# A decoder trunk's second mixer: GLA's core in batches of two token tiles and ahead of its gate, the output projection in three parts, fewer weight chunks completed by transfer

## The chip, the core and the metric

The kernel runs on one core of a Trainium2 chip. The metric is the device time of one execution in microseconds (us). TensorE (PE) multiplies, VectorE (DVE), ScalarE (ACT) and GpSimd (POOL) compute, SyncE (SP) issues most DMAs. Each engine takes its instructions strictly in the order in which the program lists them, and waits at the first one that isn't ready.

## What is computed

512 tokens of width 1024 go through two layers. Each layer is half a feed-forward block, a mixer, and another half of a feed-forward block, each added to the scaled input and layer-normed:

```python
for l in range(DEPTH):                      # DEPTH = 2, D_MODEL = 1024, D_FF = 2816
    x = layer_norm(alpha * x + 0.5 * swiglu_ffn(x, ffn1_wi[l], ffn1_wo[l]), ...)
    mix = even_mixer(x, ...) if l % 2 == 0 else odd_mixer(x, ...)
    x = layer_norm(alpha * x + mix, ...)
    x = layer_norm(alpha * x + 0.5 * swiglu_ffn(x, ffn2_wi[l], ffn2_wo[l]), ...)
```

The change is in the second layer's mixer. Its input projection feeds two groups of heads of 512 features each, RWKV-7 and GLA; their results are put side by side and multiplied by one 1024 x 1024 output matrix:

```python
def odd_mixer(x, w_in, w_out, ...):
    p = (x @ w_in).astype(jnp.float32)
    p_rk, p_gla = p[..., :RK_IN], p[..., RK_IN:]
    y_rk = rwkv7_mixer(p_rk, ...)           # per token: state <- state*w + ..., y = state @ r
    gq, gk, gv, ggd, gog = split_cols(p_gla, GLA_SIZES)
    y_gla = gla_mixer(gq, gk, gv, ggd, gog, ...)
    return jnp.concatenate([y_rk, y_gla], axis=-1).astype(x.dtype) @ w_out

def gla_mixer(q, k, v, gd, og, gB, gb, norm_g):
    log_alpha = jax.nn.log_sigmoid(gd @ gB + gb) / GLA_TAU
    ...                                     # chunks of 64 tokens, 4 heads
    attn = jnp.where(causal, einsum(q_dec, k_inv), 0.0)
    o = einsum(attn, v)
    ...
    def step(state, inp):                   # 8 chunks, one after the other
        dec, kv_c = inp
        return dec[..., None] * state + kv_c, state
    o = o + einsum(q_dec, s_prev)
    return head_norm(o, norm_g, None, GLA_NORM_EPS) * jax.nn.silu(og)
```

## The kernel before

**Products.** All large products keep float32 accuracy with three matmuls in fp32r: an operand is split into a high part and the remainder, and `hi*hi`, `lo*hi` and `hi*lo` are summed in PSUM. x is kept transposed and split as `xh` and `xl` (`hi_lo()`: ACT L166 copies the high part, DVE L167 subtracts).

**Weights.** They are streamed in chunks of 512 KB. `load()` has SP bring a chunk into `raw` (two buffers, L87). `split()` turns it into `whi` and `wlo` (five buffers): ACT L99 copies the high part, and the remainder is made in one of two ways. Normally DVE L103 subtracts. While the flag `adds` is set, which is the whole of the second mixer, ACT L101 instead writes minus the high part's source into `wlo` and POOL issues a second, accumulating transfer of the same chunk on top of it (L106), so DVE has nothing to do for it. `weights()` splits two chunks ahead of the one in use. The second mixer's chunks come in this order: `lora` (0), `gd` (1), the RWKV-7 keys, receptances and values by feature tile (2 to 13, `od_krv`), GLA's keys and queries (14 to 17), its values (18 to 21), its gate (22 to 25), and the output matrix (26 to 33, `od_w_out`).

**The second mixer, `odd(l)`.** First the projections `pj` for chunks 0 to 4 run over the tokens of the first half, then, after the last token tile is normed and transposed (`to_xT(3)`), over the second half. RWKV-7's 512 features are four tiles of 128 in two groups of two. A group goes through `keys` (gates `pw`, `pa`, norms `pn`, the bonus `pi`), `scores` (`psc`), `inverse` (a triangular inverse that DVE works out in 15 x 2 steps, L789 and L790, between block transposes L785 and L796), `natural` (transposes `ptk`, `ptb` and products `pz` on PE), `merge` (`pq`, `px`, `pwt`, `pu`: the inverse is applied; it needs the finished inverse) and `chain` (eight chunks of 64 tokens one after the other: PE `psa` L847, DVE L848, PE `pst` L854, DVE L856 and L859). `finish` norms the results and multiplies by the gate (`pyt`).

**What fills the waits.** Around these, `filler` holds a queue of generators, and `fill()` advances it by counts from the table FILL; `drain()` empties it. The first group's steps are filled with the other projections, `gla_gates`, `gla_kq` and `gla_v` (PE tile `pv`). For the second group the queue before is `gla_o` (GLA's output gate: 96 matmuls of 512 columns into `po`, then ACT L964 and DVE L965, L966 make `og`), then `gla_core` (for each of the four token tiles in turn: transposes `ptk` L992, scores `psc` L1000, a masked copy L1002 on DVE, chunk states `pkv` L1013 with DVE L1016 and L1017, outputs `po` L1023 and L1026, and their `head_norm`), then `values` (L1037 multiplies by `og`; L1040 transposes into `xh`, `xl`). A scheduler then sets the final order on each engine.

**Output projection.** `MixOut` takes the features by tiles of 128: 0 to 3 RWKV-7, 4 to 7 GLA. In each part it multiplies the tiles of that part for every token tile (PE `pout`, L161 to L163, 512 columns each) and adds the result to x on DVE (L1134 in part 0, which also scales x; L1136 in later parts). Part 0 runs as filler of the second chain; the last part, `mix.last`, also does the layer norm (L192, L194, L200, L202) and transposes x for the next block (`pst` L174, L166, L167), whose first matmul is `pgu` L128.

```python
mix = MixOut(self, (0, 1, 4), (5, 6, 7, 2, 3))
```

PSUM has eight banks: four of tag A, two of B, two of C.

Of the kernel before, what the change touches and what calls it, by code (L numbers as in the profile page):

```python
# [23 lines left out]

FILL = (
# [3 lines left out]
)  # L29


class Net:
    def __init__(self, ctx, tc, a):
# [57 lines left out]
    def split(self):  # L91
# [5 lines left out]
        for z in range(0, n, 512):  # L97
            sl = slice(z, min(n, z + 512))
            self.nc.scalar.activation(hi[:, sl], t[:, sl], AF.Copy)  # L99
            if self.adds and not fold:  # L100
                self.nc.scalar.activation(lo[:, sl], t[:, sl], AF.Copy, scale=-1.0)  # L101
            elif not fold:
                self.nc.vector.tensor_tensor(out=lo[:, sl], in0=t[:, sl], in1=hi[:, sl].bitcast(F32), op=ALU.subtract)  # L103
        if self.adds and not fold:
# [446 lines left out]

    def odd_srcs(self):
        a = self.a
        self.srcs.append((a["od_lora"][0], (8, P), 0))
        self.srcs.append((a["od_gd"], (8, 48), 32))
        for nm in ("od_krv", "od_gkq", "od_gv", "od_go"):
            for q in range(a[nm].shape[0]):
                self.srcs.append((a[nm][q], tuple(a[nm].shape[2:]), 0))
        self.out_srcs(a["od_w_out"][0], (0, 1, 4, 5, 6, 7, 2, 3))

    def odd(self, l):
        nc, a, tc = self.nc, self.a, self.tc
        V, A, T, G = nc.vector, nc.scalar, nc.tensor, nc.gpsimd
        self.adds = True
# [5 lines left out]
        with tc.tile_pool(name="od", bufs=1) as ep:  # L570
# [400 lines left out]
            def gla_start():  # L971
                nc.sync.dma_start(ng, a["gla_norm_g"].broadcast_to([P, S]))
                V.tensor_scalar(out=ng, in0=ng, scalar1=0.5, scalar2=None, op0=ALU.mult)
                at = [gp.tile([P, 2, P], F32, name=f"at{z}") for z in range(4)]
                for z in range(4):
                    G.memset(at[z], 0.0)
                return at

            qd, ki = Es, gbs

            def gla_core():
                St = gp.tile([P, 2, P], F32, name="Sg", bufs=3)
                V.memset(St, 0.0)
                for t in range(4):
                    St = yield from gla(t, St)

            def gla(t, St):
                ts = slice(t * P, (t + 1) * P)
                heads = [(f, par, slice(par * 64, par * 64 + 64), f * 256 + par * P) for f in range(2) for par in range(2)]
                p = self.psum("ptk", "A")  # L990
                for f in range(2):
                    T.transpose(p[:, f * P:(f + 1) * P], ki[f][:, ts], self.ident)  # L992
                kn = gp.tile([P, 2, P], F32, name="kn")
                A.activation(kn, p[:, :256].rearrange("p (f i) -> p f i", f=2), AF.Copy)
                yield
                pp = [self.psum("psc", "A") for _ in range(2)]
                for f in range(2):
                    for par, p in enumerate(pp):
                        rows = slice(par * 64, par * 64 + 64)
                        T.matmul(p[:, f * P:(f + 1) * P], ki[f][rows, ts], qd[f][rows, ts], start=True, stop=True)  # L1000
                for par, p in enumerate(pp):
                    V.copy_predicated(out=at[t % 2 * 2 + par], mask=m_gla.bitcast(mybir.dt.uint32).unsqueeze(1).broadcast_to([P, 2, P]), data=p[:, :256].rearrange("p (f i) -> p f i", f=2))  # L1002
                yield
                po = [self.psum("po", "A") for _ in range(2)]
                ss = []
                for z in range(2):
                    c = 2 * t + z
                    rows = slice(z * 64, z * 64 + 64)
                    ss.append(St)
                    if c < 7:  # L1010
                        p = self.psum("pkv", "A")
                        for f, par, q, i in heads:
                            T.matmul(p[q, f * P:(f + 1) * P], kn[rows, f, q], vt[t][rows, i:i + P], start=True, stop=True)  # L1013
                        pv = p[:, :256].rearrange("p (f i) -> p f i", f=2)
                        Sn = gp.tile([P, 2, P], F32, name="Sg", bufs=3)
                        V.tensor_tensor(out=Sn, in0=pv, in1=St, op=ALU.add)  # L1016
# [3 lines left out]
                for f in range(2):  # L1020
                    two = [(po[par][:, f * P:(f + 1) * P], par, q, i) for g, par, q, i in heads if g == f]
                    for o, par, q, i in two:
                        T.matmul(o, at[t % 2 * 2 + par][:, f, :], vt[t][:, i:i + P], start=True, stop=False)  # L1023
                    for z in range(2):
                        for o, par, q, i in two:
                            T.matmul(o[z * 64:z * 64 + 64], qd[f][q, t * P + z * 64:t * P + z * 64 + 64], ss[z][q, f, :], start=False, stop=True)  # L1026
                sm = ep.tile([P, 48], F32, name="sm", bufs=2)
                y = slot("kr")
                head_norm(sm, [(po[h % 2][:, h // 2 * P:(h // 2 + 1) * P], y[:, h * P:(h + 1) * P]) for h in range(4)], 1e-5)
                yg.append(y)  # L1030
                yield
                return St


# [65 lines left out]

            filler.append(mix_first())
            for t, y in enumerate(chain(grp)):
# [4 lines left out]
            for q in later:  # L1107
                rk_values(*q)
            gp.release()
            self.adds = False  # L1110
            mix.last(l, lambda nm: slot("y" if nm != "lnt" else "kr"))


# [159 lines left out]
```

## Time and profile before

| | |
|---|---|
| median of 3 runs | 2036.09 us (2035.59 to 2046.99) |
| the profiled execution | 2039.38 us, of which the span is 2037.6 us |
| PE busy in the span | 2003.2 us (98%) |
| DVE, ACT, POOL busy | 966.1 us (47%), 716.7 us (35%), 95.1 us (5%) |
| mean granted PE clock | 0.991 |
| second mixer | from about 1320 us to 1667 us of the span |

The page has one row of busy time for each engine, the span in 40 slices (the second mixer is in slices 26 to 33, counted from 1), and the chain that ended last, with the share of each engine and line. Views for a stretch of time give each engine's busy time there, the granted PE clock, which falls from 1.00 to 0.50 in places, and the DMA engines' share. A row of waits names the PE line that waited, the engine and line it waited for, the total in us, how often, and the longest.

### The profile page before, as it was taken

The numbers are of one execution on the slowest core, as the hardware profiler recorded it, in microseconds if no ns is written. First come the engines' busy times: TensorE is split into PE (matmuls) and PEld (weight loads), VectorE is DVE, ScalarE is ACT, GpSimd is POOL, SyncE is SP. The second block draws the span as 40 slices with busy tenths as digits, with TensorE's granted clock in tenths as the row PEclk, the third lists the DMA queues.
The fourth block names the chain that finished last, engine by engine and source line by source line (L and its number), as shares of the span: only waits on it lengthen the run. The fifth ranks groups of instructions, "written<-read, shape, count | busy, mean of one in ns | idle before, by whom it ended". The sixth has DMA issues, their size and how long they took to land.

```text
span 2037.6 us, 26047 instructions
## 1 busy us (share of the span) xinstructions
PE 2003.2 (98%) x10485; PEld 1661.1 (82%) x10485; DVE 966.1 (47%) x1800; ACT 716.7 (35%) x1264; POOL 95.1 (5%) x157
## 2 busy tenths in 40 slices
PE   9999999999999999999999999998999999999998
PEld 8888888876888888888988888886777788888886
DVE  4332333766784323336433333436857784323335
ACT  4332331456433322332332233166535333322330
POOL 0000000100010000000000000012111200000001
PEclk9999999999999999999999999998998999999999
DMA  5233332322223233232333332285536023333331
GB/s 177 93 101 117 95 102 83 98 93 63 72 93 115 93 97 121 93 97 65 118 99 97 114 103 94 77 213 114 132 81 157 20 84 114 96 101 114 99 98 63
DMA packets 60635, 206.64 MB, mean 101 GB/s; under 512 B 7953, under 2 KB 8417, under 8 KB 60513
## 3 DMA queue, kind: packets, MB, share of 16 engines
q1 hardware_dynamic: 56336, 189.77, 29.8%
q0 software_dynamic: 4176, 15.21, 4.0%
q8 instruction: 82, 1.34, 0.3%
q14 instruction: 41, 0.33, 0.1%
HBM read 200.75 MB, written 4.19 MB: 101 GB/s over the span
## 4 chain that ended last, share of the span: by engine, by line
PE 90%; DVE 4%; ACT 3%; DMA 2%; issue 1%; POOL 0%; POOLq 0%; SPq 0%; DVEq 0%; ACTq 0%
PE pgu L128 16%; PE pgu L129 16%; PE pgu L132 16%; PE acc L163 8%; PE acc L162 8%; PE acc L161 8%; PE pout L161 1%; PE pout L162 1%; PE pout L163 1%; DMA raw<-od_krv 1%; PE pv L152 1%; PE pst L174 1%; PE pj L128 1%; ACT whi L99 1%; PE pv L154 1%
## 5 line engine op out<-in xcount | busy, mean ns | idle before, releaser
L99 ACT ACTIVATE whi<-raw 128x512 fp32r<-128x512 f32 x661 | 380.3, 623 | 839.6 <-PE pgu L129 403.4
L103 DVE TENSOR_TENSOR wlo<-raw,whi 128x512 fp32r<-128x512 f32 x600 | 388.4, 687 | 533.4 <-ACT whi L99 507.8
L128 PE MATMUL pgu<-xh,whi 128*128 128x512 f32 (+1 forms) x1568 | 563.1, 368 | 1.5 <-ACT whi L99 1.3
L129 PE MATMUL pgu<-xl,whi 128*128 128x512 f32 (+1 forms) x1568 | 564.0, 368 | 0.0
L132 PE MATMUL pgu<-xh,wlo 128*128 128x512 f32 (+1 forms) x1568 | 353.6, 367 | 0.0
L128 PEld LDWEIGHTS pgu<-xh,whi 128*128 128x128 f32 x1568 | 294.2, 188 | 50.5 <-ACT whi L99 1.5
L129 PEld LDWEIGHTS pgu<-xl,whi 128*128 128x128 f32 x1568 | 295.2, 188 | 48.6
L132 PEld LDWEIGHTS pgu<-xh,wlo 128*128 128x128 f32 x1568 | 275.7, 189 | 48.6
L161 PE MATMUL acc<-whi,hh 128*128 128x512 f32 x704 | 274.4, 390 | 0.0
L162 PE MATMUL acc<-whi,hl 128*128 128x512 f32 x704 | 274.2, 389 | 0.0
L163 PE MATMUL acc<-wlo,hh 128*128 128x512 f32 x704 | 272.3, 390 | 0.0
L239 DVE TENSOR_TENSOR sg<-sg,pgu 128x512 f32<-128x512 f32 (+1 forms) x96 | 61.7, 643 | 335.6 <-PE pgu L132 331.4
L162 PEld LDWEIGHTS acc<-whi,hl 128*128 128x128 f32 x704 | 132.2, 188 | 27.3
L161 PEld LDWEIGHTS acc<-whi,hh 128*128 128x128 f32 x704 | 132.2, 188 | 27.2
L163 PEld LDWEIGHTS acc<-wlo,hh 128*128 128x128 f32 x704 | 132.1, 188 | 27.2
L166 ACT ACTIVATE hh<-sg 128x512 fp32r<-128x512 f32 (+1 forms) x96 | 57.3, 596 | 121.5 <-DVE sg L239 121.5
L196 POOL TENSOR_SCALAR rs<-mv 128x1 f32<-128x1 f32 x24 | 13.7, 571 | 1507.5 <-DVE mv L194 1507.5
L238 ACT ACTIVATE sg<-pgu 128x512 f32<-128x512 f32 (+1 forms) x96 | 53.7, 560 | 56.0 <-PE pgu L132 55.4
L128 PE MATMUL pj<-xh,whi 128*128 128x512 f32 (+2 forms) x184 | 65.4, 372 | 0.0
L166 ACT ACTIVATE xh<-pst 128x512 fp32r<-128x512 f32 x48 | 27.5, 596 | 106.6 <-PE pst L174 106.5
L129 PE MATMUL pj<-xl,whi 128*128 128x512 f32 (+2 forms) x184 | 62.7, 357 | 0.0
L167 DVE TENSOR_TENSOR hl<-sg,hh 128x512 fp32r<-128x512 f32 (+1 forms) x96 | 61.6, 641 | 0.6 <-ACT hh L166 0.5
(342 smaller groups left out, 2006.5 us busy)
## 6 DMA issues: line engine op xcount, KB each, us to landing
raw<-ffn_wi SPq DMA_DIRECT2D x176, 512.0 KB, 3.5
raw<-ffn_wo SPq DMA_DIRECT2D x88, 512.0 KB, 3.5
raw<-od_krv SPq DMA_DIRECT2D x12, 512.0 KB, 4.6
wlo<-od_krv POOLq DMA_DIRECT2D x12, 512.0 KB, 7.6
raw<-ev_qk SPq DMA_DIRECT2D x8, 512.0 KB, 3.5
raw<-ev_rg SPq DMA_DIRECT2D x8, 512.0 KB, 3.4
raw<-ev_w_out SPq DMA_DIRECT2D x8, 512.0 KB, 3.5
raw<-od_w_out SPq DMA_DIRECT2D x8, 512.0 KB, 4.2
```

The costliest lines, as they stand in the source:

```text
L99: self.nc.scalar.activation(hi[:, sl], t[:, sl], AF.Copy)
L103: self.nc.vector.tensor_tensor(out=lo[:, sl], in0=t[:, sl], in1=hi[:, sl].bitcast(F32), op=ALU.subtract)
L128: mm(o, hi[:, kt, :n], self.xh[:, kt, t0:t1], start=kt == 0, stop=False)
L129: mm(o, hi[:, kt, :n], self.xl[:, kt, t0:t1], start=False, stop=lo is None and kt == 7)
L132: mm(o, lo[:, kt, :n], self.xh[:, kt, t0:t1], start=False, stop=kt == 7)
L161: mm(o, ah, hi[:, cs], start=first and i == 0, stop=False)
L162: mm(o, al, hi[:, cs], start=False, stop=False)
L163: mm(o, ah, lo[:, cs], start=False, stop=last and i == len(lhs) - 1)
L166: self.nc.scalar.activation(hi, src, AF.Copy)
L167: self.nc.vector.tensor_tensor(out=lo, in0=src, in1=hi.bitcast(F32), op=ALU.subtract)
L238: nc.scalar.activation(sg, pp[f, 0][:, t0:t1], AF.Silu)
L239: nc.vector.tensor_tensor(out=sg, in0=sg, in1=pp[u][:, t0:t1], op=ALU.mult)
```

## The change

It has three parts, all in the second mixer.

- `gla_core` works on two token tiles at a time: one `ptk` bank for four transposes, two `psc` banks for sixteen scores, masked copies of 512 columns in place of 256, two `pkv` banks that hold all four chunk states of the batch, then the two tiles' outputs. `filler` takes `gla_core`, then `gla_o`, then `values`, all queued behind the second group's `inverse`; the count at that place of FILL is 22 in place of 19, and later counts change too.
- The output projection has three parts: tiles (0, 1, 4), then (5, 6, 7), then (2, 3). The first two are filler of the second chain.
- `adds` is a range of chunk numbers in place of a flag: chunks 8 to 31 of the second mixer are completed by transfer. Chunks 2 to 7 (`od_krv` for the first two feature tiles) and the last two of the output matrix are subtracted on DVE. Before, the flag was set when `odd` began and cleared before `mix.last`: 2 to 7 were completed by transfer, and of the output matrix chunks 26 to 30. As built, the adding transfers of `od_krv` go from 12 to 6 and L101 on `od_w_out` covers one chunk more.

```diff
-    3, 1, 2, 2, 3, 2, 1, 3, 2, 1, 0, 1, 1, 3, 0, 0, 6, 3, 3, 5, 6, 4, 2, 9, 0, 1, 19, 8, 0, 1, 4, 2,
-    1, 3, 1, 0, 1, 2, 2, 3, 1, 4, 0, 1, 1, 1, 2, 0, 1,
+    3, 1, 2, 2, 3, 2, 1, 3, 2, 1, 0, 1, 1, 3, 0, 0, 6, 3, 3, 5, 6, 4, 2, 9, 0, 1, 22, 6, 6, 2, 2, 2,
+    2, 1, 1, 1, 1, 1, 1, 1, 1, 1, 1, 1, 1, 1, 1, 1, 1,
...
-            if self.adds and not fold:
+            if self.nsp in self.adds and not fold:
                 self.nc.scalar.activation(lo[:, sl], t[:, sl], AF.Copy, scale=-1.0)
...
     def odd_srcs(self):
+        n = len(self.srcs)
+        self.adds = range(n + 8, n + 32)
...
-                for t in range(4):
-                    St = yield from gla(t, St)
+                for t0 in (0, 2):
+                    St = yield from gla(t0, St)
+            def gla(t0, St):
+                ts = [slice((t0 + i) * P, (t0 + i + 1) * P) for i in range(2)]
                 p = self.psum("ptk", "A")
+                for i in range(2):
+                    for f in range(2):
+                        T.transpose(p[:, (2 * i + f) * P:(2 * i + f + 1) * P], ki[f][:, ts[i]], self.ident)
...
                 for par, p in enumerate(pp):
+                    V.copy_predicated(out=at[par], mask=m_gla..., data=p.rearrange("p (t f i) -> p t f i", t=2, f=2))
                 yield
+                pp = [self.psum("pkv", "A") for _ in range(2)]
...
+                for c in range(2 * t0, 2 * t0 + 4):
                     ss.append(St)
                     if c < 7:
+                        V.tensor_tensor(out=Sn, in0=pp[z][:, i * 256:i * 256 + 256]..., in1=St, op=ALU.add)
                         V.tensor_tensor(out=Sn, in0=Sn, in1=Dg[...], op=ALU.mult)
                         St = Sn
...
-            mix = MixOut(self, (0, 1, 4), (5, 6, 7, 2, 3))
+            mix = MixOut(self, (0, 1, 4), (5, 6, 7), (2, 3))
...
-            filler += [gla_o()]
+            filler += [gla_core(), gla_o(), values()]
             fill()
-            filler += [gla_core(), values()]
             merge(grp)
...
-                yield from mix.part(0, "A")
+                for i in range(2):
+                    yield from mix.part(i, "A")
...
-            self.adds = False
```

**PE beside the second inverse.** Before, PE has the gate's matmuls (`po<-whi,xh` and its two companions) between the transposes and `pz` products of `natural`. These rows are from the middle of that stretch:

```order
L154 MATMUL po<-wlo,xh 128x512
L773 MATMUL pz<-KV,SC 64x64 x16
L759 MATMUL ptk<-ident,KRV 128x128 x4
L152 MATMUL po<-whi,xh 128x512
L153 MATMUL po<-whi,xl 128x512
```

In the changed kernel the core's batches stand there (L994, L1003, L1015, L1032, L1036). This is the beginning of the second batch:

```order
L994 MATMUL ptk<-ident,ga 128x128 x4
L1003 MATMUL psc<-E_10211,ga 128x128
L1003 MATMUL psc<-E_10212,ga 128x128
L1003 MATMUL psc<-E_10211,ga 128x128
L1003 MATMUL psc<-E_10212,ga 128x128
L1003 MATMUL psc<-E_10211,ga 128x128
L1003 MATMUL psc<-E_10212,ga 128x128
L1003 MATMUL psc<-E_10211,ga 128x128
L1003 MATMUL psc<-E_10212,ga 128x128
L1015 MATMUL pkv<-kr,kn 64x128 x16
L1032 MATMUL po<-kr,at_11717 128x128
L1036 MATMUL po<-Sg,E_10211 64x128
```

Behind those twelve rows stand ten `pq`, then the rest of that batch's outputs, twenty-one `pq`, and only then the gate's matmuls; `gla_o`'s 96 matmuls have moved from beside the inverse to behind it.

**DVE at the second inverse.** Before, its 30 steps (L789, L790) stand nearly one behind the other (between them are two L167 and two memsets). In the changed kernel L790 and L791 are the same steps, and the core's instructions stand between them, here from the middle:

```order
L790 TENSOR_TENSOR ZU<-ZU 64x210
L1022 TENSOR_TENSOR Sg<-pkv,Sg 128x256
L791 TENSOR_TENSOR ZU<-ZU 64x10x21
L1023 TENSOR_TENSOR Sg<-Sg,Dg 128x256
L790 TENSOR_TENSOR ZU<-ZU 64x198
L1022 TENSOR_TENSOR Sg<-pkv,Sg 128x256
L883 BN_STATS sm<-po 128x6 x3
```

The second batch's masked copies are the two L1005 at the end of the inverse, one ahead of its last step and one behind its three closing transposes (L794 and L797):

```order
L1005 COPY_PREDICATED at_11717<-cst,psc 128x512
L791 TENSOR_TENSOR ZU<-ZU 64x30
L794 STREAM_TRANSPOSE WT<-ZU 32x32x32
L797 STREAM_TRANSPOSE SC<-ZU 32x32x32 x2
L1005 COPY_PREDICATED at_11718<-cst,psc 128x512
L1022 TENSOR_TENSOR Sg<-pkv,Sg 128x256
L1023 TENSOR_TENSOR Sg<-Sg,Dg 128x256
```

So the whole first batch's DVE work, and one of the second's copies, have moved into the inverse.

**PE in the second chain.** Before, a step of the chain from `psa` to the next `psa` is filled with GLA's core and transposes of its results:

```order
L847 MATMUL psa<-St,WT 64x128
L1040 MATMUL pyt<-ident,kr 128x128 x4
L854 MATMUL pst<-KV,BK 128x128 x2
L870 MATMUL py<-KV,SC 64x64 x3
L866 MATMUL py<-St,R 64x128 x2
L870 MATMUL py<-KV,SC 64x64 x4
L1040 MATMUL pyt<-ident,kr 128x128 x4
```

In the changed kernel nine `pout` stand between `psa` (L848 there) and `pst` (L855), and eight or nine behind the `py` of each token tile:

```order
L848 MATMUL psa<-St,WT 64x128
L161 MATMUL pout<-whi,xh 128x512
L162 MATMUL pout<-whi,xl 128x512
L163 MATMUL pout<-wlo,xh 128x512
L161 MATMUL pout<-whi,xh 128x512
L162 MATMUL pout<-whi,xl 128x512
L163 MATMUL pout<-wlo,xh 128x512
L161 MATMUL pout<-whi,xh 128x512
L162 MATMUL pout<-whi,xl 128x512
L163 MATMUL pout<-wlo,xh 128x512
L855 MATMUL pst<-KV,BK 128x128 x2
```

Between the last product of the last chunk (`py`, L870 before, L871 after) and the first `pgu` of the next block, 161 `pout` remain before and 74 after.

More of the change, by code (lines that the diff above doesn't have):

```diff
@@ L54, in __init__ @@
         self.raw = {}
-        self.adds = False
+        self.adds = range(0)
         self.spl = {}
@@ L103, in split @@
                 self.nc.vector.tensor_tensor(out=lo[:, sl], in0=t[:, sl], in1=hi[:, sl].bitcast(F32), op=ALU.subtract)
-        if self.adds and not fold:
+        if self.nsp in self.adds and not fold:
             self.nc.gpsimd.dma_start(lo[:, :n].rearrange("p (a b) -> p a b", a=shape[0]), ap, accum_op=ALU.add)
@@ L973, in gla_start @@
                 V.tensor_scalar(out=ng, in0=ng, scalar1=0.5, scalar2=None, op0=ALU.mult)
-                at = [gp.tile([P, 2, P], F32, name=f"at{z}") for z in range(4)]
-                for z in range(4):
-                    G.memset(at[z], 0.0)
+                at = [gp.tile([P, 2, 2, P], F32, name=f"at{par}") for par in range(2)]
+                for par in range(2):
+                    G.memset(at[par], 0.0)
                 return at
@@ L996, in gla @@
                 pp = [self.psum("psc", "A") for _ in range(2)]
[L997 to L1000, printed above, removed]
+                for i in range(2):
+                    for f in range(2):
+                        for par, p in enumerate(pp):
+                            rows = slice(par * 64, par * 64 + 64)
+                            T.matmul(p[:, (2 * i + f) * P:(2 * i + f + 1) * P], ki[f][rows, ts[i]], qd[f][rows, ts[i]], start=True, stop=True)
@@ L1001, in gla @@
                 for par, p in enumerate(pp):
[L1002 removed]
+                    V.copy_predicated(out=at[par], mask=m_gla.bitcast(mybir.dt.uint32).unsqueeze(1).unsqueeze(1).broadcast_to([P, 2, 2, P]), data=p.rearrange("p (t f i) -> p t f i", t=2, f=2))
                 yield
[L1004 removed]
+                pp = [self.psum("pkv", "A") for _ in range(2)]
@@ L1005, in gla @@
+                for i in range(2):
+                    for f in range(2):
+                        for par in range(2):
+                            for z, p in enumerate(pp):
+                                rows, q = slice(z * 64, z * 64 + 64), slice(par * 64, par * 64 + 64)
+                                j = f * 256 + par * P
+                                T.matmul(p[q, (2 * i + f) * P:(2 * i + f + 1) * P], kn[rows, i, f, q], vt[t0 + i][rows, j:j + P], start=True, stop=True)
                 ss = []
-                for z in range(2):
-                    c = 2 * t + z
-                    rows = slice(z * 64, z * 64 + 64)
+                for c in range(2 * t0, 2 * t0 + 4):
@@ L1009, in gla @@
                     ss.append(St)
                     if c < 7:
[L1011 to L1016, printed above, removed]
+                        i, z = (c - 2 * t0) // 2, c % 2
@@ L1017, in gla @@
+                        Sn = gp.tile([P, 2, P], F32, name="Sg", bufs=5)
+                        V.tensor_tensor(out=Sn, in0=pp[z][:, i * 256:i * 256 + 256].rearrange("p (f i) -> p f i", f=2), in1=St, op=ALU.add)
                         V.tensor_tensor(out=Sn, in0=Sn, in1=Dg[:, :, c:c + 1].broadcast_to([P, 2, P]), op=ALU.mult)
                         St = Sn
-                    yield
[L1020 to L1031, printed above, removed]
+                yield
+                for i in range(2):
+                    po = [self.psum("po", "A") for _ in range(2)]
+                    for f in range(2):
+                        two = [(po[par][:, f * P:(f + 1) * P], par, slice(par * 64, par * 64 + 64)) for par in range(2)]
+                        for o, par, q in two:
+                            j = f * 256 + par * P
+                            T.matmul(o, at[par][:, i, f, :], vt[t0 + i][:, j:j + P], start=True, stop=False)
+                        for z in range(2):
+                            for o, par, q in two:
+                                u = (t0 + i) * P + z * 64
+                                T.matmul(o[z * 64:z * 64 + 64], qd[f][q, u:u + 64], ss[2 * i + z][q, f, :], start=False, stop=True)
+                    sm = ep.tile([P, 48], F32, name="sm", bufs=2)
+                    y = slot("kr")
+                    head_norm(sm, [(po[h % 2][:, h // 2 * P:(h // 2 + 1) * P], y[:, h * P:(h + 1) * P]) for h in range(4)], 1e-5)
+                    yg.append(y)
+                    yield
@@ L1098, in mix_first @@
                     rk_values(i, slice(0, S))
-                yield from mix.part(0, "A")
+                for i in range(2):
+                    yield from mix.part(i, "A")
             filler.append(mix_first())
@@ L1109, in odd @@
             gp.release()
-            self.adds = False
             mix.last(l, lambda nm: slot("y" if nm != "lnt" else "kr"))
```

12 lines of the change are left out of this document (3 added, 9 removed).

## The prediction

> **What bounds the kernel now.** I start with the page's busy times and chain.
>
> ```profile
> PE 2003.2 (98%) x10485; PEld 1661.1 (82%) x10485; DVE 966.1 (47%) x1800; ACT 716.7 (35%) x1264; POOL 95.1 (5%) x157
> PE 90%; DVE 4%; ACT 3%; DMA 2%; issue 1%; POOL 0%; POOLq 0%; SPq 0%; DVEq 0%; ACTq 0%
> ```
>
> TensorE is the bound nearly everywhere. The change neither adds nor removes PE work: the same matmuls come in another order. So it can only move time in which PE idles or runs slowly. I therefore look for these in the second mixer, first from the last key score of the second group (1526.85, called T0) to the next block's first `pgu` (1667.10): beside the inverse, behind it, in the chain, and in the tail. Columns: length, then busy us of PE, PEld, DVE, ACT and POOL with their instructions, granted clock, DMA share, GB/s.
>
> ```profile
> 1526.85:1537.91 11.06, 11.06 (x55) 9.16 (x55) 10.36 (x23) 5.47 (x11) 0.86 (x1) 1.00 0.32 71
> 1537.91:1562.20 24.29, 24.29 (x229) 20.00 (x228) 22.05 (x49) 15.90 (x29) 4.27 (x8) 1.00 0.84 198
> 1562.20:1580.60 18.40, 16.13 (x247) 12.61 (x240) 9.12 (x15) 7.16 (x14) 1.08 (x2) 0.72 0.50 154
> 1580.60:1624.30 43.70, 40.54 (x376) 30.33 (x374) 32.23 (x121) 15.68 (x41) 11.95 (x28) 1.00 0.07 15
> 1624.30:1667.10 42.80, 42.25 (x199) 34.12 (x199) 34.05 (x73) 11.52 (x25) 5.87 (x10) 1.00 0.15 50
> ```
>
> PE is busy throughout the inverse's 35.35 us. In all 140.25 us it idles 2.27 + 3.16 + 0.55 = 6.0 us. Second, the granted clock, in windows of the same kind:
>
> ```profile
> 1339.50:1342.90 3.40, 1.31 (x11) 1.10 (x10) 1.55 (x6) 1.57 (x4) 1.39 (x2) 1.00 1.04 277
> 1342.90:1346.30 3.40, 3.40 (x18) 3.38 (x18) 0.13 (x2) 0.00 (x0) 0.00 (x0) 0.50 1.06 251
> 1383.90:1387.30 3.40, 1.12 (x2) 0.29 (x2) 3.30 (x6) 3.40 (x8) 0.93 (x1) 1.00 0.41 119
> 1387.30:1394.10 6.80, 6.16 (x12) 3.79 (x13) 5.85 (x10) 4.13 (x8) 1.16 (x2) 0.50 1.03 243
> 1418.00:1424.80 6.80, 6.58 (x26) 5.99 (x27) 5.98 (x8) 5.04 (x11) 2.01 (x3) 0.50 0.53 119
> 1561.40:1564.80 3.40, 1.64 (x90) 1.42 (x84) 2.84 (x4) 1.07 (x2) 0.86 (x1) 0.99 1.02 358
> 1564.80:1575.00 10.20, 10.20 (x98) 7.65 (x93) 3.44 (x5) 2.79 (x5) 0.00 (x0) 0.50 0.47 132
> 1611.00:1614.40 3.40, 2.15 (x16) 1.58 (x15) 2.11 (x7) 3.20 (x10) 1.80 (x5) 1.00 0.02 5
> 1614.40:1617.80 3.40, 3.40 (x23) 2.65 (x21) 3.34 (x19) 1.19 (x4) 2.20 (x6) 1.00 0.00 0
> ```
>
> Where PE is busy 1.1 to 1.6 us of a window of 3.4, the clock is 0.50 for the next 3.4 to 10.2 us; after 2.15 us it stays. Half of such a stretch is lost: 1.7, 3.4, 3.4 and 5.1 us at the four places. With the second half's idle time that makes 6.0 + 5.1 = 11.1 us lost there. Third, PE's waits from 1330 to 1425:
>
> ```profile
> PE pn L701 <- ACT wk L697: 3.4, 2, 2.5
> PE pw L688 <- DVE wk L728: 2.2, 1, 2.2
> PE pj L132 <- DMA wlo<-od_krv: 2.1, 1, 2.1
> PE pa L692 <- ACT wk L690: 1.6, 1, 1.6
> PE pi L726 <- ACT wk L724: 0.8, 1, 0.8
> ```
>
> **The change part by part: chunks 2 to 7.** Twelve L101 on ACT and six accumulating transfers go; twelve L103 on DVE come.
>
> ```profile
> wlo<-od_krv POOLq DMA_DIRECT2D x12, 512.0 KB, 7.6
> raw<-od_krv SPq DMA_DIRECT2D x12, 512.0 KB, 4.6
> L101 ACT ACTIVATE wlo<-raw 128x512 fp32r<-128x512 f32 x26 | 15.5, 618 | 0.0
> L103 DVE TENSOR_TENSOR wlo<-raw,whi 128x512 fp32r<-128x512 f32 x600 | 388.4, 687 | 533.4 <-ACT whi L99 507.8
> ```
>
> The DMA engines are full in the first window (share 1.04), and each remainder lands 7.6 us after its issue. Without six of them the `pj` wait of 2.1 us ends, and with it the half clock behind it (1.7). ACT gets 12 x 0.618 = 7.4 us back, and its chain of gates feeds `pa`, `pi` and `pn`: 1.6 + 0.8 + 0.9 (of the two `pn` waits the shorter). If these go, the window at 1383.90 no longer idles and 3.4 us of half clock go too. The wait of `pw` is on DVE, which gets 12 x 0.687 = 8.2 us more; its 2.2 us may go, because the weights come earlier, or stay. In sum 2.1 + 1.7 + 1.6 + 0.8 + 0.9 + 3.4 = 10.5 without `pw`, 12.7 with it. The longer `pn` wait (2.5) and the half clock at 1418 lie behind the third feature tile's gates, whose chunks are still completed by transfer; they stay. I take **-10.5**. The ends: -16 if that stall halves too (2.5 + 3.4, by half: 3.0), and -3 if only the `pj` wait goes because DVE's 8.2 us come late for the gates.
>
> **GLA's core under the inverse.** The inverse is DVE's:
>
> ```profile
> L790 DVE TENSOR_TENSOR ZU<-ZU 64x30 f32<-64x30 f32 (+14 forms) x30 | 9.9, 330 | 1.0
> L789 DVE TENSOR_TENSOR ZU<-ZU 64x30 f32<-64x30 f32 (+14 forms) x30 | 9.9, 329 | 1.0
> L1002 DVE COPY_PREDICATED at<-cst,psc 128x256 f32<-128x256 uint32 x8 | 3.2, 439 | 1.6 <-PE psc L1000 1.5
> L1016 DVE TENSOR_TENSOR Sg<-pkv,Sg 128x256 f32<-128x256 f32 x7 | 2.9, 420 | 1.1 <-PE pkv L1013 1.0
> L882 DVE BATCH_NORM_STATS2 sm<-po 128x6 f32<-128x128 f32 x16 | 3.7, 286 | 2.6 <-PE po L1026 2.4
> L884 DVE BATCH_NORM_AGGREGATE sm<-sm 128x2 f32<-128x6 f32 x28 | 3.0, 154 | 0.0
> ```
>
> Inserted ahead of its end are three masked copies of twice 256 columns (3 x 0.75, an estimate between 0.44 and 0.88), four pairs of L1022 and L1023 (8 x 0.42, starts some 0.36 apart), eight norm statistics (8 x 0.286, starts 0.22 apart) and eight aggregates (8 x 0.154): 2.2 + 2.9 + 1.8 + 0.9, about 7.6 us with their rounding. DVE stood idle 35.35 - 10.36 - 22.05 = 2.9 us there, of which I let 2.4 take some up. The inverse ends 7.6 - 2.4 = 5.2 us later, at T0 + 40.5.
>
> PE meanwhile loses its cover:
>
> ```profile
> L152 PE MATMUL po<-whi,xh 128*128 128x512 f32 x27 | 10.8, 401 | 0.0
> L1023 PE MATMUL po<-kr,at 128*128 128x128 f32 x32 | 6.4, 307 | 0.0
> L1026 PE MATMUL po<-Sg,E 64*64 64x128 f32 x64 | 5.3, 294 | 0.0
> ```
>
> 81 of `gla_o`'s 96 matmuls ran there, at 0.2275 us from start to start (an estimate: 10.8 us of L152 alone counts overlap): 18.4 us. In their place come batch one and batch two as far as the first ten `pq`, which wait for the inverse: by the rows above half of 6.4 + 5.3 and the scores, states and transposes, 13.2 us with the waits inside a batch. So PE has 35.35 - 18.4 + 13.2 = 30.2 us of work, 28.2 when I walk the starts one by one, against 40.5. It idles **12.3** (10.3 by the first count). Then batch two's outputs must be normed before the gate's PSUM banks come free: another **3.4** (one aggregate, POOL's four small steps and ACT's scaling take about 2 us). After such idling the clock halves for at least the 3.4 us of the shortest row, up to 10.2: 1.7 to 5.1 lost, I take **2.6**. `og` and `values` come in one burst on DVE ahead of the chain's first operand: four L965, L966 and L1037 of 0.69 us each, 8.3 us of DVE, against PE with only `pyt` left to do: **3.2** idle.
>
> **The chain and the tail.** With nine `pout` (nine times 0.2275, 2.0 us) between `psa` and `pst`, the chain's waits on DVE and ACT vanish and PE is busy there. But 87 `pout` (161 less 74), 19.8 us, have gone from the tail:
>
> ```profile
> L162 PE MATMUL pout<-whi,xl 128*128 128x512 f32 x54 | 21.4, 396 | 0.0
> L1136 DVE TENSOR_TENSOR x<-x,pout 128x512 f32<-128x512 f32 x7 | 4.7, 682 | 1.4 <-PE pout L163 1.4
> L192 DVE BATCH_NORM_STATS2 st<-x 128x6 f32<-128x512 f32 x7 | 4.7, 688 | 0.1
> L200 DVE SCALAR_TENSOR_TENSOR kr<-x,mv,y 128x512 f32<-128x512 f32 x6 | 4.2, 748 | 0.1
> L202 DVE SCALAR_TENSOR_TENSOR x<-kr,rs,y 128x512 f32<-128x512 f32 x6 | 4.5, 747 | 0.9 <-POOL rs L197 0.9
> ```
>
> DVE was busy 34.05 of that stretch's 42.80 us, and the third part adds eight more additions of 0.68 to it or to the chain. Per token tile the tail has two each of L1136, L192, L200, L202 and L167, about 7.3 us; four tiles make 29, with `finish` of the last tile and the next block's L103 35 us. PE has 42.25 - 19.8 - 1.5 (what moved over the border) = 20.9 us to do. The tail takes 35 us and PE idles **14**.
>
> **Sum.** Second half: lost after 12.3 + 3.4 + 2.6 + 3.2 + 14 = 35.5, before 11.1: **+24** (from +14, where the inverse is lengthened by only 2 and the tail takes 29, to +34, with 10.2 us windows of half clock twice and a tail of 40). With the first half 24 - 10.5 = +13.5, so 2039.38 + 13.5 = 2052.9 for the profiled execution (its span of 2037.6 and 1.8 around it). That one lies 3.3 above the median of the runs; against the median I say **2050**.
>
> A rule of the Trainium skill bears on this. "TensorE: Matmul & The Clock Gate", section "What's actually happening", has the clock fall to half after an idle window of about 3.4 us and come back after a busy one. The windows above agree on the length and on 0.50, but here 1.1 to 1.6 us of work did not prevent it. Read strictly, the page's rule would spare the tail, where no idle piece is that long (14 us in four tiles, about 3.5 each and in pieces): by it the time stays at 2050, by the falling rows it is the first rival's.
>
> **Rivals.** *The tail runs at half clock* (slower). PE would be busy 20.9 of 35 us, 2.03 us in a window of 3.4: between the rows that fall (1.64) and the row that stays (2.15). If it falls, the 20.9 us become up to 41.8, more than DVE's 35: the tail is 6.8 longer, and the next `pgu` begin with 3.4 us at 0.50 (1.7), and the longer half clock behind the inverse adds 2.5. Price 11, **2061**. It decides from 2.03 being above or below the gate's point, which lies between 1.64 and 2.15. *The first half gains nothing*: the waits of `pa`, `pi`, `pn` hang on chains through DVE, which has 8.2 us more to do; only the `pj` wait goes: 2050 + 7.5 = **2057.5**. *DVE is less in the way* (no slower): GLA's operations fit between the inverse's dependent steps, and the tail keeps up with its additions at 29 us. The second half is then +14 or less, the first -10.5 to -16: 2036 + 14 - 10.5 = 2039.6 down to **2034**. *PE never waits for DVE* (faster): nothing is idle in the second half (-11.1), the first gives -12.7: **2012**. The inverse with DVE busy 32.4 of 35.35 us speaks against it. *The change does not do what it says*: the rows of the order do show it.
>
> **How the numbers follow.** Forecast 2050 (2043 to 2056): 0.46. Tail at half clock 0.20, first half without gain 0.10, DVE less in the way 0.17, PE never waiting 0.07. One per cent is 20.4 us, about what a measurement of this kernel can tell from no change: 2015.7 and 2056.5. Faster by more: 0.07. Slower by more: the tail's 0.20, half of the 0.10 and 0.04 of the forecast's upper edge: 0.29. Between: 0.64. The range leaves out PE never waiting and the far ends of both sides: 2030 to 2066.
>
> **What would show it.** Right: PE idle for some 10 to 12 us near T0 + 28 waiting for the inverse's transposes, the first `gla_o` matmul near T0 + 48, no wait of `pj` on `od_krv`, no half clock at 1387, chain waits near nothing, a tail of 35 us with DVE over 90% busy, and T0 to `pgu` about 164. Wrong: PE busy beside the inverse, a tail under 25 us, or first-half waits that merely change names.

## The result and the profile after

The changed kernel takes 2064.01 us (median; 2059.75 to 2066.45) against 2040.62 us (2035.59 to 2046.99) in the runs beside it. The ratio is 1.0105, 95% interval 1.0075 to 1.0135: about 1% slower. The profiled execution took 2066.45 us with a span of 2064.7; before, 2039.38 and 2037.6. Two executions of the later runs, 7135 us of the kernel before and 2222 us of adds_dense, were slow at mean granted clocks of 0.267 and 0.845 and are in none of the ratios.

The page of the changed kernel, busy times and chain:

```profile
PE 2024.0 (98%) x10493; PEld 1676.9 (81%) x10493; DVE 978.0 (47%) x1814; ACT 711.6 (34%) x1252; POOL 89.5 (4%) x150
PE 88%; DVE 6%; ACT 2%; DMA 2%; issue 1%; POOL 0%; POOLq 0%; DVEq 0%; SPq 0%; ACTq 0%
```

PE is busy 20.8 us longer with the same work, which is the sign of a slower clock rather than of waiting (the mean granted clock is 0.982, 0.991 before); DVE's share of the chain has gone from 4% to 6%. The changed kernel's second half, in windows as before: `pv` to T0 + 10.8, the inverse, batch two's outputs, the gate and merge, the chain, the tail, and the first 22.9 us of the next block:

```profile
1523.90:1534.70 10.80, 10.80 (x55) 8.94 (x55) 10.10 (x23) 5.45 (x10) 0.86 (x1) 1.00 0.35 73
1534.70:1566.70 32.00, 26.14 (x262) 19.49 (x260) 28.66 (x74) 11.71 (x24) 5.64 (x11) 0.73 0.36 109
1566.70:1572.00 5.30, 4.46 (x28) 3.13 (x32) 4.25 (x16) 0.00 (x0) 0.00 (x0) 0.50 0.00 0
1572.00:1608.00 36.00, 35.61 (x359) 27.85 (x360) 11.26 (x25) 17.38 (x35) 5.97 (x11) 0.89 0.42 103
1608.00:1657.80 49.80, 46.49 (x297) 36.12 (x295) 30.82 (x90) 14.19 (x34) 7.26 (x14) 0.97 0.27 64
1657.80:1689.50 31.70, 22.73 (x103) 17.28 (x103) 28.73 (x63) 10.08 (x22) 4.69 (x10) 0.95 0.30 85
1689.50:1712.40 22.90, 21.89 (x159) 21.29 (x158) 10.63 (x19) 5.76 (x10) 1.18 (x2) 0.85 0.07 22
```

Beside the inverse PE now idles 5.9 us and the clock averages 0.73; in the tail it idles 9.0 us while DVE is busy 28.73 of 31.70; and the next block begins at 0.85, where the same stretch before ran at full clock:

```profile
1667.10:1690.00 22.90, 22.90 (x194) 22.90 (x193) 14.68 (x27) 10.71 (x20) 0.79 (x2) 1.00 0.40 126
```

What PE waits for there, changed kernel, T0 to the next block:

```profile
PE pst L174 <- DVE x L202: 5.9, 1, 5.9
PE psa L848 <- DVE St L860: 3.3, 1, 3.3
PE po L1036 <- DVE Sg L1023: 2.5, 2, 2.2
PE po L1032 <- DVE at L1005: 2.1, 1, 2.1
PE pout L161 <- DVE y L907: 1.7, 1, 1.7
```

Every one of them is DVE: the core's states and masked copies queued between the inverse's steps, the burst ahead of the chain's second `psa`, and the layer norm of the last token tile. Ahead of the inverse, 1340 to 1425, two waits are left of five:

```profile
PE pn L702 <- ACT wk L698: 2.5, 1, 2.5
PE pa L693 <- ACT wk L691: 1.3, 1, 1.3
```

By stages, from the traces of all runs, one execution of each kernel (us). A chain begins with its first `psa`, the inverse ends with DVE's closing transposes, the tail begins behind the last `py`. "Half" is the half clock's length in the first chain and from T0 to `pgu`, divided by two, an estimate of the most that it cost PE:

| run | first `pj` to first chain | first chain to T0 (half) | T0 to inverse's end | to second chain | second chain | tail | T0 to `pgu` (half) | `pgu` to the end |
|---|---|---|---|---|---|---|---|---|
| before | 151.1 | 47.3 (0) | 35.3 | 20.8 | 41.4 | 42.9 | 140.3 (5.1) | 370.4 |
| changed | 140.7 | 52.6 (6.8) | 42.8 | 41.0 | 50.1 | 31.7 | 165.6 (18.8) | 375.2 |
| adds_only | 140.1 | 46.5 (0) | 35.3 | 21.7 | 54.4 | 46.4 | 157.8 (23.9) | 370.4 |
| adds_undone | 149.9 | 47.3 (0) | 42.2 | 40.5 | 50.9 | 30.1 | 163.7 (18.7) | 375.6 |
| gate_first | 140.6 | 46.5 (0) | 35.3 | 20.1 | 64.3 | 31.6 | 151.3 (8.8) | 375.0 |
| two_parts | 142.5 | 52.6 (6.8) | 42.9 | 41.1 | 46.6 | 36.7 | 167.4 (25.6) | 370.4 |
| adds_dense | 140.3 | 52.6 (6.8) | 34.8 | 18.3 | 41.3 | 47.0 | 141.4 (1.7) | 370.4 |
| adds_small | 140.2 | 46.5 (0) | 34.8 | 20.2 | 53.9 | 48.7 | 157.6 (17.0) | 370.4 |
| before_dense | 150.4 | 47.3 (0) | 34.8 | 18.3 | 41.3 | 42.8 | 137.3 (0) | 370.4 |
| after_dense | 140.7 | 46.5 (0) | 45.2 | 39.2 | 49.9 | 32.7 | 167.0 (16.5) | 375.7 |
| dense_to_30 | 139.0 | 52.6 (6.8) | 34.8 | 18.3 | 41.3 | 42.8 | 137.2 (0) | 370.4 |
| dense_more | 141.3 | 47.3 (0) | 34.8 | 18.3 | 41.3 | 42.8 | 137.3 (0) | 370.4 |
| dense_batches | 143.3 | 52.5 (6.8) | 34.8 | 20.4 | 56.9 | 37.9 | 150.0 (10.2) | 370.4 |

From the first two rows the 27.1 us between the two spans follow: 2.1 ahead of the mixer (its first `pj` is at 1330.6 against 1328.5, work that the change doesn't touch), -10.4, +5.3, +25.3, and +4.8 behind `pgu`.

### The profile page after: what moved, and what is told of

Its sections match the earlier page's. It is cut to its first block, busy times and chain, and to the rows that moved or that the text cites. A ratio compares the mean times of both kernels' runs of the same rounds, so it can differ in the third digit from the quotient of the medians.

```text
span 2064.7 us, 26060 instructions
## 1 busy us (share of the span) xinstructions
PE 2024.0 (98%) x10493; PEld 1676.9 (81%) x10493; DVE 978.0 (47%) x1814; ACT 711.6 (34%) x1252; POOL 89.5 (4%) x150
## 4 chain that ended last, share of the span: by engine, by line
PE 88%; DVE 6%; ACT 2%; DMA 2%; issue 1%; POOL 0%; POOLq 0%; DVEq 0%; SPq 0%; ACTq 0%
PE pgu L129 16%; PE pgu L128 16%; PE pgu L132 16%; PE acc L162 8%; PE acc L161 8%; PE acc L163 8%; PE pout L161 1%; PE pout L162 1%; PE pout L163 1%; PE pst L174 1%; PE po L152 1%; DVE ZU L791 1%; DVE wlo L103 1%; DVE ZU L790 1%; PE po L153 1%
## 5 line engine op out<-in xcount | busy, mean ns | idle before, releaser
L103 DVE TENSOR_TENSOR wlo<-raw,whi 128x512 fp32r<-128x512 f32 x610 | 394.9, 687 | 536.2 <-ACT whi L99 508.9
L167 DVE TENSOR_TENSOR hl<-sg,hh 128x512 fp32r<-128x512 f32 (+1 forms) x96 | 61.6, 642 | 1.6 <-ACT hh L166 1.5
```

The lines of the kernel that those rows point to most:

```text
L167: self.nc.vector.tensor_tensor(out=lo, in0=src, in1=hi.bitcast(F32), op=ALU.subtract)
```

## The experiments

**One part at a time.** The kernels are named by their runs. Theory A was the prediction's, sized by the two traces; B, C and D put the loss on one part or another. First the new range of transfers alone, on the kernel before:

```diff
-        self.adds = True
+        self.adds = range(n + 8, n + 32)     # in odd_srcs, tested by chunk in split()
```

> The kernel before with only the new range of chunks completed by transfer (8 to 31). Theory A (the working of the prediction, sized by the two traces: pj's wait on od_krv and the waits of the gates pn, pw, pi go, which moves the fourth tile's gates 8 us forward in the changed kernel, and the first chain may give some of it back at half clock): 3 to 9 us faster than before, 2032 to 2038 where before has 2041; no wait of pj on a remainder, no half clock near 1343 and a shorter one near 1387. Rival B (ACT's and the transfers' relief is taken back by DVE's twelve subtractions): within 2 us of before.

It is slower: 2047.51 us, ratio 1.0035 (1.0018 to 1.0051). Yet the gain of the first half is there, 151.1 to 140.1 us, and the waits are those expected (1340 to 1425):

```profile
PE pn L702 <- ACT wk L698: 2.5, 1, 2.5
PE pa L693 <- ACT wk L691: 0.9, 1, 0.9
```

What takes it back stands behind the second inverse, in matmuls that this kernel shares with the one before: 13.0 us more in the second chain and 3.5 in the tail. In adds_only, the window with `pwt`, `pkv` and `pu`, and the stretch behind it:

```profile
1561.30:1564.70 3.40, 2.78 (x78) 2.43 (x78) 3.06 (x7) 1.79 (x4) 0.86 (x1) 1.00 0.55 130
1564.70:1602.20 37.50, 35.73 (x227) 25.37 (x219) 16.27 (x58) 5.53 (x15) 5.05 (x12) 0.50 0.09 17
```

The same view of the kernel before:

```profile
1581.80:1624.30 42.50, 39.34 (x362) 29.42 (x361) 31.14 (x120) 15.29 (x40) 11.95 (x28) 1.00 0.04 9
```

The same chain ran at full clock in one kernel and for 37.5 us at half clock in the other. PE was busy 35.73 of those 37.50 us, more than before's 39.34 of 42.50 in proportion, and the clock did not come back. (The two are not like for like: at half clock a matmul takes longer, and the 35.73 us hold 227 matmuls where the 39.34 hold 362.) The Trainium skill ("TensorE: Matmul & The Clock Gate", "What's actually happening") has the full rate return after one busy window of about 3.4 us; of the eleven windows here ten are busy from end to end by this profile, and they did not suffice, so it is the measurement that counts. Both theories failed as written: A's gain was real and was lost elsewhere, in the second chain and the tail, and DVE's twelve subtractions (B) were not what took it.

The range undone in the changed kernel:

```diff
-        self.adds = range(n + 8, n + 32)
+        self.adds = range(n + 2, n + 31)
```

> The changed kernel with the old range of chunks (2 to 30) completed by transfer; the core's batches, the queue and the three parts stay. Theory A: the second half costs its 25 us and the start of the next block 4 to 5 without any gain ahead of it, so 26 to 33 us slower than before, about 2070, and 3 to 9 us slower than the changed kernel. Rival B: within 2 us of the changed kernel.

2067.58 us, 1.0126 (1.0105 to 1.0147): 3.6 us slower than the changed kernel by the medians, at the lower end of A, though the two intervals overlap. Its first half lacks the 9 us, but its first chain, too, lacks the 13.7 us of half clock.

The gate first again, with the batches behind it; the filler counts at that place go with it (19, 8, 5 for 22, 6, 6, and later ones):

```diff
-            filler += [gla_core(), gla_o(), values()]
+            filler += [gla_o()]
             fill()
+            filler += [gla_core(), values()]
```

> The changed kernel with the gate's matmuls queued beside the inverse again, and GLA's batches behind it (counts of the fillers 19, 8, 5, 2 ...); batches, three parts and the new range stay. Theory A (the cost is PE's idle time beside the lengthened inverse, 5 to 9 us, and the half clock that starts there, 30.7 us of it against 10.2 before): 12 to 20 us faster than the changed kernel, 2044 to 2052, PE fully busy until the inverse ends, inverse about 35 us. Rival C (the cost is the short tail behind an early projection): at most 5 us faster than the changed kernel, since the tail and the half clock at the next block's start stay.

2049.94 us, 1.0054 (1.0028 to 1.0080): 14 us faster than the changed kernel. The inverse takes 35.3 us again, and T0 to the second chain 55.4 instead of 83.8; the chain, which now holds the core, gives 14.2 of these 28.4 back (64.3 against 50.1). C falls by the size of the gain, though the short tail and the slow start of the next block stay as it said (31.6 and 375.0); A holds, and the move of the core ahead of the gate is the largest single cost. The executions vary from 2043 to 2069 us, the fastest at a mean granted clock of 0.990 and the slowest at 0.979; the one traced has 20.5 us of half clock in two pieces from the tail into the next block, and where the others lost theirs is not known.

And the output projection in two parts again, only the first of them filling the chain:

```diff
-            mix = MixOut(self, (0, 1, 4), (5, 6, 7), (2, 3))
+            mix = MixOut(self, (0, 1, 4), (5, 6, 7, 2, 3))
```

> The changed kernel with the output projection in two parts, (0,1,4) and (5,6,7,2,3), only the first of them filling the chain. Theory A: the tail has 120 output matmuls again and ends with PE; the 9 us of PE's idle time there and the half clock of the next block's start (10.2 us of it, 4 to 5 us) go, but the second chain, with fewer output matmuls, has waits of 3 to 6 us: 6 to 12 us faster than the changed kernel, 2052 to 2058. Rival C (the tail is the whole cost): 20 us or more faster, 2044 or less. Rival D (only the place of the core counts): within 3 us of the changed kernel.

2061.57 us, 1.0089 (1.0069 to 1.0109): 2.4 us faster by the medians, within D's 3 us and with overlapping intervals. The next block starts at full clock again (370.4 against 375.2), but the tail, which I expected to end with PE, takes 5.0 us more than with three parts, and a half clock of 13.7 us lies across its start.

**The clock by itself.** If half clock is the loss, matmuls that compute nothing but hold the clock should bring time back. They write a PSUM bank that the next matmul overwrites:

```diff
+            def dense(o, n):
+                for _ in range(n):
+                    T.matmul(o, self.xh[:, 0, :P], self.xh[:, 0, :o.shape[-1]], start=True, stop=True)
                 p = self.psum("px", "C")
+                dense(p, wait)                         # 6 in the second merge
                         p = self.psum(nm, "C")
+                        dense(p, each if nm == "pu" else 0)      # 4
```

> The kernel with only the new range of chunks, and in the second group's merge 14 matmuls that compute nothing (128x512, operands from xh, their bank is overwritten at once): six ahead of px, where PE waits 1.75 us, and four ahead of each pu. Theory A (the clock gate: 8 to 12 us gained ahead of the second inverse are lost behind it to a half clock of 37.5 us that starts in a window of 64x64 matmuls and that the chain's small matmuls don't end; wide matmuls keep the window busy): the half clock behind the inverse is gone or under 10 us, PE does 1.8 to 3.2 us more, 12 to 20 us faster than the range alone, 2028 to 2036, faster than before. Rival B (the new range costs the time elsewhere): 2 to 3 us slower than the range alone.

2036.56 us, 0.9961 (0.9944 to 0.9977): 11 us faster than the range alone by the medians (some 15 by the two ratios, each against the runs of the kernel before beside it), and faster than before. The second chain's 41.4 us are back, all at full clock:

```profile
1575.80:1617.20 41.40, 38.24 (x350) 28.73 (x349) 30.60 (x118) 15.35 (x40) 11.99 (x28) 1.00 0.01 4
```

That is A, near the lower end of its 12 to 20 us. It does not hang on the one trace: the mean granted clock is 0.982 to 0.986 in the twelve executions with the range alone and 0.990 to 0.996 in the eleven here. The trace shows two things that A had not reckoned with: a half clock of 13.7 us in the first chain, and a new wait in the tail (below).

> As the kernel with 14 idle matmuls, but in place of the four wide ones ahead of each pu, every 64x64 matmul of pu is issued three times (32 more per pu, about 1.2 us each by the starts of 0.036 us). The six ahead of px stay. Theory A (it is width that holds the clock, not PE being busy): the half clock behind pu stays or comes back in most executions, so at least 8 us slower than with the wide ones. Rival E (a matter of where the chain lies against the gate's windows, or of any work there): within 3 us of the wide ones.

```diff
-                        dense(p, each if nm == "pu" else 0)
...
+                                    for _ in range(3 if nm == "pu" and each else 1):
+                                        T.matmul(p[q, i:i + 64], l, r, start=True, stop=True)
```

2046.62 us, 1.0028 (1.0013 to 1.0043): 10 us slower than with wide ones. With narrow matmuls in the same place the clock does not last through the chain. Where it fell is not where A put it, though:

```profile
1564.10:1567.60 3.50, 3.50 (x117) 3.50 (x114) 1.41 (x4) 0.60 (x1) 0.00 (x0) 1.00 1.01 224
1567.60:1571.00 3.40, 3.40 (x49) 2.48 (x45) 2.19 (x7) 0.82 (x2) 0.00 (x0) 1.00 0.08 16
1571.00:1574.40 3.40, 1.59 (x15) 1.07 (x13) 1.91 (x10) 1.07 (x4) 1.67 (x4) 0.99 0.00 0
1574.40:1601.70 27.30, 25.64 (x158) 18.24 (x160) 11.84 (x42) 3.25 (x9) 1.81 (x5) 0.50 0.00 1
```

The window of the second repeated `pu` and the one behind it kept it at 1.00; a later one with 1.59 us of work, in the chain itself, let it fall, and it again stayed down for 27.3 us. So the size is A's, and width as the cause is not shown by itself: how the windows of the clock lie against the chain matters as well.

> The kernel before with the same 14 idle matmuls. Theory A: the 10.2 us of half clock behind its inverse go (5.1 gained), 1.8 to 3.2 us of matmuls come: 0 to 4 us faster than before. Rival B: 2 to 3 us slower than before.

2037.51 us, 0.9989 (0.9972 to 1.0005): no difference that can be told, 3.0 us less from T0 to `pgu` (140.3 to 137.3), with no half clock there. In the one trace of it the kernel before does not fall in its chain, so the idle matmuls have little to give it there; the gain of adds_dense needs both edits.

> The changed kernel with five idle matmuls of 128x512 ahead of each token tile's outputs in GLA's core (20, 4.6 us), where PE waits for DVE beside and behind the second inverse. Theory A (half of the second half's loss is the half clock of 30.7 us that these waits start): the half clock there goes or is under 10 us; 6 to 13 us faster than the changed kernel, 2051 to 2058, and the rest of the loss, PE's waits for DVE themselves, stays. Rival F (the waits alone are the loss): 0 to 4 us slower than the changed kernel.

```diff
                     po = [self.psum("po", "A") for _ in range(2)]
+                    dense(po[0], 5)
```

2063.54 us, 1.0102 (1.0087 to 1.0117): as the changed kernel. The half clock beside the inverse went only from 30.7 to 23.9 us, so this does not tell A from F. It does show that DVE does not set the inverse's end alone: PE's additional work moved it from 42.8 to 45.2 us, and DVE's idle time up to there rose from 4.0 to 5.5. Some of DVE's operations between the inverse's steps wait for PE, so more work ahead of them on PE holds up the steps behind them; in the changed kernel the second of these rows, from T0 to the inverse's end, has 1.4 us of it (the first is the masked copies'):

```profile
L1005 DVE COPY_PREDICATED at<-cst,psc 128x512 f32<-128x512 uint32 x4 | 2.9, 730 | 0.1
L883 DVE BATCH_NORM_STATS2 sm<-po 128x6 f32<-128x128 f32 x8 | 2.0, 289 | 1.4 <-PE po L1036 1.4
```

**A faster version.** In adds_dense PE has this wait in its tail, on the one chunk that the new range completes by transfer and the old one subtracted:

```profile
PE pout L163 <- DMA wlo<-od_w_out: 3.2, 1, 3.2
```

> The new range without its last chunk (8 to 30 completed by transfer, 31 subtracted again), with the 14 idle matmuls. In the run with 14 idle matmuls PE waits 3.2 us for the accumulating transfer of an od_w_out chunk, and its tail is 47.0 us against 42.9 before. Theory A (that wait is chunk 31's): no wait of pout on a remainder, tail about 43 us, 3 to 4 us faster than with chunk 31 by transfer, 2031 to 2034. Rival (the wait moves to another engine or chunk): within 1 us.

```diff
-        self.adds = range(n + 8, n + 32)
+        self.adds = range(n + 8, n + 31)
```

2030.26 us, 0.9947 (0.9926 to 0.9968): 6.3 us faster by the medians (about 3 by the ratios, whose intervals overlap), 4.2 of it in the traced tail (47.0 to 42.8). The wait is gone, and what is left in that stretch is small:

```profile
PE pst L861 <- DVE KV L855: 0.9, 1, 0.9
PE pout L161 <- DVE x L1142: 0.6, 1, 0.6
PE pyt L905 <- ACT yn L897: 0.3, 1, 0.3
```

> As the kernel with the range 8 to 30 and 14 idle matmuls, and 14 more: eight ahead of the third feature tile's pn, where PE waits 2.5 us, and six ahead of the last psa of the first chain, where it waits 1.5 us. Theory A (idle matmuls in a wait cost nothing and keep the clock): the half clock of 6.8 us near 1408 and that of 13.7 us in the first chain go, 3.4 and, where it occurs, 6 us: 3 to 9 us faster than with 14. Rival (a stretch that was at full clock in half of the executions gains nothing, and the matmuls cost their 3 us): within 2 us, or slower.

```diff
                 pn = self.psum("pn")
+                dense(pn, 8 if ft == 2 else 0)
...
                     p = self.psum("psa", "C")
+                    dense(p, wait if c == 7 else 0)      # 6 in the first chain
```

2029.31 us, 0.9930 (0.9912 to 0.9948), the lowest median of all, but only 1 us below the one with 14, which is the rival's size and no certain difference, though the two profiles differ by 3.0 from the first `pj` to `pgu` (325.8 and 328.9). The half clocks near 1408 and in the first chain are gone from this execution, which has two of 3.4 us elsewhere (at 1382 and 1457). The mean granted clock is 0.996 to 0.998 in all six executions, against 0.991 to 0.995 with 14: the clock was gained and the time hardly. And the stretch of the third tile's `pn` runs at 1.00:

```profile
1401.00:1420.00 19.00, 17.88 (x113) 13.16 (x115) 16.73 (x27) 17.76 (x30) 3.16 (x5) 1.00 0.32 70
```

> As the kernel with the range 8 to 30 and 14 idle matmuls, with GLA's core in batches of two token tiles, queued behind the gate as before, two parts of the output projection and the old filler counts: of the change only the batching and the range are left. Theory A (the batching itself only shortens DVE's masked copies, 8 of 256 columns for 4 of 512, about 0.7 us, and moves the inverse not at all): within 3 us of the one with the core tile by tile, inverse 35 us. Rival G (the batching lengthens the second chain, since more of the core comes ahead of the first psa): 4 us or more slower.

```diff
-                for t in range(4):
-                    St = yield from gla(t, St)
+                for t0 in (0, 2):
+                    St = yield from gla(t0, St)
```

2044.34 us, 1.0009 (0.9993 to 1.0025): 14 us slower than tile by tile, G. (The edit is against dense_to_30.) Its second chain takes 56.9 us against 41.3, with a half clock of 17.1 us across its end and more waiting, the longest on the results' copy:

```profile
PE pyt L905 <- ACT yn L897: 4.6, 1, 4.6
PE psa L854 <- DVE St L866: 4.0, 4, 1.5
```

Whether the longer chain is the batches' own doing or that of the old filler counts, which were made for twenty steps of the core (five for each token tile) and now meet ten, was not tried.

## Why the prediction was right, and where it was wrong

- **The time.** 2050 with a range to 2066 was forecast, 2064 came: inside, near the upper end, and past the 1% that I had given 0.29. Against the runs beside it the change costs 23.4 us where 13.9 were forecast. For the profiled execution the sum gave 2052.9 and 2066.45 came; of the 13.6 us between them 5.3 stand in the first chain, 4.8 behind `pgu` and 2.1 ahead of the mixer, none of which the sum had priced, so that the range's width covered them is luck. The direction and the main loss, from T0 to `pgu`, were right: 164 forecast, 165.6 measured. That these agree so well is luck too: PE idles 19.4 us there where 32.9 were forecast, and the half clock costs up to 18.8 where I had 2.6.
- **Chunks 2 to 7, -10.5.** 151.1 to 140.7, -10.4, and 8 to 12 in every run with that range. The waits of `pj`, `pw`, `pn` (the shorter) and `pi` are gone as worked out; `pa` kept 1.3 and 3.4 us of half clock stayed with it. The step failed in what follows it, which the sum put at nothing: a half clock of 13.7 us in the first chain, whose matmuls the change leaves as they are, took 5.3 back. In the changed kernel it starts behind a window with 2.11 us of work:

```profile
1498.30:1501.70 3.40, 2.11 (x15) 1.53 (x15) 2.03 (x9) 1.44 (x4) 0.46 (x2) 1.00 0.76 140
1501.70:1515.40 13.70, 13.70 (x60) 10.52 (x60) 4.12 (x16) 2.46 (x5) 1.18 (x3) 0.50 0.00 1
```

  Adds_only has the same work there, 2.12 us of it in a window, and stays:

```profile
1493.00:1496.40 3.40, 2.12 (x13) 1.53 (x12) 2.03 (x9) 1.44 (x4) 0.58 (x2) 1.00 0.75 145
1496.40:1510.10 13.70, 13.69 (x104) 11.02 (x105) 7.47 (x25) 4.97 (x11) 2.58 (x5) 1.00 0.22 51
```

  Five of the thirteen profiles have this half clock, in the same place. All twelve without idle matmuls there have the same 1.3 us of idle PE ahead of the chain's last four `psa`. What differs is where the clock's own windows lie: in every trace it changes only on a grid of 3.41 us, and the window between two of these steps that holds the start of this idle time begins 3.4 to 4.2 us ahead of these `psa` in the seven that stay, 2.2 to 3.3 us in the five that fall. The three with the old range are among the seven. So in these traces the place of the chain against the windows sorts the two, and not the busy time of PE alone; this was read from the traces afterwards, one execution of each, and was not tried.
- **The core under the inverse.** The inverse became 7.5 us longer, not 5.2: DVE's busy time up to its end grew by 6.4 us (32.4 to 38.8) where I had 7.6 (a masked copy of 512 columns took 0.73 us for my 0.75; my four terms add up to 7.8 as written, and eight aggregates of 0.154 are 1.2, not 0.9), but DVE's idle time there, 42.8 - 10.1 - 28.7 = 4.0 us, did not shrink from 2.9 by the 2.4 that I let it. PE's idle time beside and behind it is 5.9 + 0.8 us where I had 12.3 + 3.4, and the half clock costs up to 15.4 (30.7 us of it) where I had 2.6. The sum of the two is near (22.1 against 18.3) and the split is wrong: at half clock PE's work fills the time in which I let it idle. The burst was sized rightly, 3.3 for 3.2, but the chain's first `psa` went ahead of it and PE waited at the second.
- **The tail.** 31.7 us and 9.0 idle for 35 and 14; DVE 91% busy, as said. It did not run at half clock throughout, so that rival fell, but its end did: the idle time was not in the four pieces of about 3.5 us that I had, but in one wait of 5.9 us for the last layer norm among others, and 10.2 us at 0.50 begin within it, at 1686.0, and last into the next block. That cost 4.8 where the rival had 1.7 and the forecast nothing.
- **The rivals.** *The tail at half clock* lay nearest with 2061, but by another cause. Its point between 1.64 and 2.15 us of PE's busy time does not exist as such: 2.12 stayed and 2.11 fell in the rows above, 2.78 fell in adds_only, and 1.77 stayed in the changed kernel's tail:

```profile
1668.98:1672.40 3.42, 1.77 (x8) 1.16 (x7) 3.03 (x8) 1.59 (x4) 0.00 (x0) 1.00 0.60 161
1672.40:1675.80 3.40, 3.16 (x14) 2.25 (x13) 3.26 (x7) 0.00 (x0) 0.81 (x2) 1.00 0.84 280
```

  *The first half gains nothing* fell. *DVE is less in the way* and *PE never waits* fell too. What I lacked was a rival of the kind that decided most: a half clock that starts in one place and stays through work that is unchanged.

So by taking parts of the change back, and by the medians: the core ahead of the gate costs 14 us, the third part of the output projection 2.4, and the new range is worth about 3.5. Only the first stands clear of the runs' spread, and the three leave some 10 of the 23 us without an owner. Part of them may be the batches, which cost 14 us where they were tried on dense_to_30, with the old counts. How much of the changed kernel's loss beside the inverse is PE's waiting and how much the half clock that it starts is open too, since after_dense hardly moved either.

## What to carry to other kernels

Beside a long serial stretch on one engine put work that needs nothing of that engine; work that shares its queue lengthens the stretch and removes the cover at once (here 42.8 us for 35.3). After an edit compare the granted clock stage by stage, also where the code is unchanged, before the edit is judged: here a real gain of 11 us showed as a loss of 7 until a few wide matmuls, in waits or ahead of a run of narrow ones, kept the clock up. And take each part of a change back by itself: the best versions keep of it only the new range, without its last chunk, and have idle matmuls beside it.

## What the hardware did that I had not expected

- A half clock that begins ahead of a chain of small dependent matmuls can last through it: 37.5 us with PE busy 95% of the time, 27.3 us in another run, while the same chain at full clock keeps it with 93% busy.
- PE's busy time in a window does not tell whether the clock falls. A window with 2.78 of 3.40 us, mostly of 64x64 matmuls, was followed by half clock, one with 1.77 us of `pout` 512 columns wide was not, and in the first chain 2.11 fell and 2.12 stayed. The row of 2.15 us in the prediction was not cut at the clock's own steps.
- The steps of the clock lie on a grid of 3.41 us, which does not start with the program: the one near 418 us, in nine profiles, begins anywhere from 417.3 to 419.7.
- Fourteen idle matmuls of 128x512, at most 3.2 us of PE's time by an estimate (14 times 0.2275), were worth 11 us or more in the kernel with the new range and nothing certain in the one before.
